# The next tile's h: root along partitions by way of DRAM, squares behind softmaxes, x loaded in pairs

## The chip, the core and the metric

One core of a Trainium2 chip runs the whole layer. The metric is the time of one execution in device microseconds (us).

## What is computed

One decoder layer on x of 2048 tokens by 1024 channels, all in float32:

```python
h = rms_norm(x, pre_norm_g)                      # h = x * rsqrt(mean(x*x) + EPS) * g, by token
proj = h @ w_in
a_u, a_v, sq, sk, sv, mq, z = jnp.split(proj, split_at, axis=-1)
y_a = chunked_spatial_gating(gelu(a_u), gelu(a_v), ...)     # group A
y_b = sliding_window_attention(sq, sk, sv, sinks, bias)     # group B, 4 heads, window 128
y_c = memory_cross_attention(mq, mk, mv)                    # group C, 4 heads, 256 memory tokens
y = jnp.concatenate([y_a, y_b, y_c], -1) * silu(z)
x = x + rms_norm(y @ w_out, post_norm_g)
```

The change touches only how h is made for the tiles of tokens after the first.

## The kernel before

The tokens are worked on in four tiles `t` of 512 (TS). `hTs` holds two tiles of h, transposed: channels along partitions in eight chunks k of 128, tokens along the free axis. Every float32 operand of a big product is split into a rounded part (made on ACT) and the rest (made on DVE), and a product of 8 chunks is 24 matmuls. So h takes three steps a chunk: a first step on DVE (x times g times the token's root), a rounding on ACT, a subtraction on DVE.

A tile runs through *units* of the weights: V (four banks of PSUM, `vps`), SV, K, Q, MQ, then eight Z and four U. After each quarter of a unit from the second Q on, `slot()` is called. Slots are numbered through the tile, 68 in tile 0 and 60 in the others, and a slot issues the jobs that a table put there, and the next stage of an attention unit. The attention of a tile is 12 units: n = 0 to 3 windows (names with `_b`), then `3_1` and the like for head 3, half 1 of the memory attention (`_c`). A unit has three stages, some slots apart: the logits `l_c`, their maximum `nm_c`, exp and normalised `L_c`; the transposes `tp_c` and their split `pT_c`; the product `o_c` and its sum `OC`. For t > 0 the eight memory units begin at slots 27, 30 and so on to 48, their transposes stand 7 slots later and their products 11. These small products, and the broadcast below, share four buffers of PSUM (`ps_t`) in turn; the units share four others.

PE and SP run in the order in which the program is written. The instructions of DVE, ACT and POOL are ordered by a scheduler that goes by its own estimate of when each is ready; within an engine they then run strictly in that order. `queue_aside` sets a few instructions straight behind a softmax. SP issues nearly all DMAs, in order: where one has to wait for its data or its buffer, those behind it wait as well. A load of weights (`whl`) waits for the buffer of the unit before, so SP keeps pace with PE unit by unit. Stores of results (`yd`, from the tiles `Z_z` and `a`) and of prepared weights of the last layer part (`wo_...`) are issued some slots after their data are due (`store_later`). The prepared weights are made in the hT that the next tile will use, so each of its chunks is free only when a store has read it.

For the next tile's h, `token_stats` loads 512 by 512 pieces of x's rows (`xs`, eight of 128 x 512, two buffers of the tag `xk`) and squares each on ACT with a sum over the row. The square has no fixed place on ACT. `rms_rstd` makes the root of the sums (`rsa_x` on DVE, `rsr_x` on POOL), a number per token along partitions. `along` turns it into a row on all partitions: four broadcasts and transposes on PE into a PSUM buffer (`bc`), copied by DVE to `bcs`. Then `load_h` loads chunk by chunk of x transposed (`xk`, the same two buffers) and makes h. In tiles t > 0 the pieces start at slots 22 to 36, the broadcast stands at slot 46, the chunks at 47 to 57; in tile 0 at 40 to 54, 58, and 59 to 66. All eight chunks are made before V of the next tile.

Of the kernel before, what the change touches and what calls it, by code (L numbers as in the profile page):

```python
# [15 lines left out]
P = 128  # L16
# [19 lines left out]
STORE_AFTER = 6  # L36
TURN_SLOT = 30
A_SLOTS0, A_SLOTS = (14, 5, 8, 13, 33, 8, 13), (7, 5, 8, 13, 27, 7, 11)


@with_exitstack
def kernel(
# [33 lines left out]
    def f32(ap):  # L76
        return ap.bitcast(F32)

    def split(hi, lo, src, lo_engine=None):
        nc.scalar.copy(hi, src)  # L80
        (lo_engine or nc.vector).tensor_tensor(lo, src, f32(hi), ALU.subtract)  # L81
# [101 lines left out]

    def token_stats(t):

        ss = tiny.tile([P, 4], F32, tag="ss", name=f"ss_{t}")
        if t > 0:
            parts = tiny.tile([P, 2, 4], F32, tag="ss2", name=f"ss2_{t}")
            for i in range(4):
                for c in range(2):  # L190
                    xs = sp.tile([P, TS], F32, tag="xk", name=f"xs_{t}_{i}_{c}", bufs=2)
                    nc.sync.dma_start(xs, x[t * TS + i * P : t * TS + (i + 1) * P, c * 512 : c * 512 + 512])
                    nc.scalar.activation(xs, xs, AF.Square, accum_out=parts[:, c, i : i + 1])
                    if i < 3 or c == 0:
                        yield
            nc.vector.tensor_tensor(ss, parts[:, 0], parts[:, 1], ALU.add)
            yield rms_rstd(ss, D, EPS, f"x{t}", "x")
            return
# [8 lines left out]
        yield rms_rstd(ss, D, EPS, f"x{t}", "x")  # L207

# [9 lines left out]

    def split_h(xk, t, k, bcs):

        hT = hTs[t % 2]
        g = g_pre[:, k : k + 1]
        if bcs is None:
            nc.scalar.mul(hT[:, 0, k, :], xk, g)
            nc.vector.scalar_tensor_tensor(hT[:, 1, k, :], xk, g, f32(hT[:, 0, k, :]), ALU.mult, ALU.subtract)
        else:
            nc.vector.scalar_tensor_tensor(xk, xk, g, bcs, ALU.mult, ALU.mult)
            split(hT[:, 0, k, :], hT[:, 1, k, :], xk)
# [174 lines left out]
    def window_unit(t, c, S, O, done):  # L403
# [27 lines left out]
        for h in range(4):  # L431
            last = nc.scalar.activation(Lc[:, h, : P + 1], Lc[:, h, : P + 1], AF.Exp, bias=nm[:, h : h + 1],  # L432
                                        accum_out=den[:, h : h + 1])
# [32 lines left out]
    def memory_unit(t, h, cc, S, O, done):  # L466
# [14 lines left out]
        for e in range(2):  # L481
            scale = late["rstd"][:, 2 * cc + e : 2 * cc + e + 1] if t == 0 else 1.0
            last = nc.scalar.activation(p[:, e, :], lg[:, e, :], AF.Exp, bias=nm[:, e : e + 1], scale=scale,  # L483
                                        accum_out=den[:, e : e + 1])
# [90 lines left out]
    def first_sums(place):  # L575
# [606 lines left out]
```

## Time and profile before

| | before |
|---|---|
| time, median of 3 runs (lowest to highest) | 785.67 us (781.81 to 788.67) |
| the profiled execution's own time | 783.76 us |
| its span, and what lies around it | 781.8 us, 1.96 us |
| granted clock of PE over the span | 0.996 |
| PE busy | 759.6 us, 97% of the span |
| DVE, ACT, POOL busy | 73%, 51%, 20% |
| DMA | 199.48 MB, mean 255 GB/s |

The tiles begin with V at 5, 174, 322 and 472 us of the span; the last product begins at 618 us. A row of the timeline has the start in us from the beginning of the span, the length of the merged piece, the engine, the line, the operation, what it writes and reads, its shape, and how many instructions; in brackets stands how long the engine was idle before it and what it waited for. Matmuls are pipelined, so that the time that one takes from the others is the step from start to start, and the same goes for DVE. A row of waits has the total, the number and the longest. A row of DMA issues ends with the median time from issue to landing.

### The profile page before, as it was taken

The numbers are of one execution on the slowest core, as the hardware profiler recorded it, in microseconds if no ns is written. First come the engines' busy times: TensorE is split into PE (matmuls) and PEld (weight loads), VectorE is DVE, ScalarE is ACT, GpSimd is POOL, SyncE is SP. The second block draws the span as 40 slices with busy tenths as digits, with TensorE's granted clock in tenths as the row PEclk, the third lists the DMA queues.
The fourth block names the chain that finished last, engine by engine and source line by source line (L and its number), as shares of the span: only waits on it lengthen the run. The fifth ranks groups of instructions, "written<-read, shape, count | busy, mean of one in ns | idle before, by whom it ended". The sixth has DMA issues, their size and how long they took to land.

```text
span 781.8 us, 10715 instructions
## 1 busy us (share of the span) xinstructions
PE 759.6 (97%) x3788; PEld 638.2 (82%) x3788; DVE 567.6 (73%) x1052; ACT 397.4 (51%) x879; POOL 157.8 (20%) x141
## 2 busy tenths in 40 slices
PE   8999999899999999999999999999999999999994
PEld 7878987787888888888887788888888878888883
DVE  6497998795658789744796796748976325697787
ACT  7686666653654656355455553544434233343442
POOL 4565543220502210041031000201300000010013
PEclk9999999999999999999999999999999999999998
DMA  8856557736875996947989769864464699818717
GB/s 326 296 205 245 184 204 256 272 123 273 314 261 210 320 316 227 343 165 224 371 292 309 260 218 379 339 261 161 142 216 178 237 388 402 322 55 322 270 32 291
DMA packets 54133, 199.48 MB, mean 255 GB/s; under 512 B 5275, under 2 KB 5824, under 8 KB 43840
## 3 DMA queue, kind: packets, MB, share of 16 engines
q1 hardware_dynamic: 53552, 198.20, 70.1%
q8 instruction: 30, 0.49, 0.2%
q10 hardware_dynamic: 528, 0.59, 0.2%
q14 instruction: 23, 0.19, 0.1%
HBM read 142.15 MB, written 56.63 MB: 254 GB/s over the span
## 4 chain that ended last, share of the span: by engine, by line
PE 70%; DMA 13%; DVE 11%; ACT 3%; issue 2%; POOL 1%; SPq 0%; POOLq 0%; DVEq 0%; ACTq 0%
PE g_z L247 14%; PE v L674 9%; PE g_u L247 7%; PE Y_S L1030 6%; PE Y L1030 5%; PE g_q L247 4%; PE g_mq L247 4%; DMA xs<-in_x 4%; PE X L1030 3%; PE X_S L1030 3%; DMA yd<-Z_z 2%; DMA split_d<-whl 2%; PE g_sv L247 2%; PE g_k L247 2%; PE gm L351 1%
## 5 line engine op out<-in xcount | busy, mean ns | idle before, releaser
L247 PE MATMUL g_z<-hT,whl 128*128 128x512 f32 x768 | 193.7, 396 | 0.0
L247 PEld LDWEIGHTS g_z<-hT,whl 128*128 128x128 f32 x768 | 138.3, 188 | 25.0
L81 POOL TENSOR_TENSOR whl<-wraw,whl 128x1024 fp32r<-128x1024 f32 x30 | 73.6, 2456 | 139.8 <-ACT whl L80 92.8
L247 PE MATMUL g_u<-hT,whl 128*128 128x512 f32 x384 | 97.7, 396 | 0.0
L674 PE MATMUL v<-whl,hT 128*128 128x512 f32 x384 | 88.9, 391 | 2.2 <-DVE sc_z L254 1.7
L674 PEld LDWEIGHTS v<-whl,hT 128*128 128x128 f32 x384 | 71.6, 188 | 18.6 <-DVE sc_z L254 2.1
L247 PEld LDWEIGHTS g_u<-hT,whl 128*128 128x128 f32 x384 | 69.2, 188 | 12.7
L80 ACT CAST whl<-wraw 128x1024 fp32r<-128x1024 f32 (+1 forms) x39 | 40.0, 1027 | 25.5 <-DMA wraw<-in_wst 6.8
L928 POOL TENSOR_TENSOR r<-a,mhalf 128x1 f32<-128x1 f32 x16 | 13.7, 856 | 191.1 <-DVE a L926 178.2
L447 POOL TENSOR_SCALAR_AFFINE_SELECT pp_b<-po_b 128x512 fp32r<-128x512 f32 x30 | 19.9, 663 | 143.3 <-ACT po_b L80 143.3
L247 PE MATMUL g_q<-hT,whl 128*128 128x512 f32 x192 | 45.9, 394 | 0.0
L1030 PE MATMUL Y<-hT,yop 128*128 128x512 f32 x192 | 44.5, 391 | 0.8 <-DVE yop L903 0.8
L247 PE MATMUL g_mq<-hT,whl 128*128 128x512 f32 x192 | 44.7, 389 | 0.0
L1030 PE MATMUL Y_S<-hT,yop_S 128*128 128x512 f32 x192 | 44.2, 389 | 0.0
L1030 PEld LDWEIGHTS Y<-hT,yop 128*128 128x128 f32 x192 | 35.8, 188 | 9.2 <-DVE yop L903 1.7
L1030 PEld LDWEIGHTS Y_S<-hT,yop_S 128*128 128x128 f32 x192 | 36.0, 188 | 7.5
L247 PEld LDWEIGHTS g_q<-hT,whl 128*128 128x128 f32 x192 | 35.7, 188 | 7.8 <-issue 0.5
L247 PEld LDWEIGHTS g_mq<-hT,whl 128*128 128x128 f32 x192 | 35.9, 188 | 7.3
L483 ACT ACTIVATE L_c<-l_c,nm_c 128x256 f32<-128x256 f32 x48 | 22.3, 469 | 28.7 <-DVE nm_c L478 28.6
L432 ACT ACTIVATE Lc_b<-Lc_b,nm_b 128x129 f32<-128x129 f32 x64 | 25.1, 394 | 18.9 <-DVE nm_b L430 18.8
L157 POOL TENSOR_TENSOR rsr_v<-rsa_v,mhalf 128x4 f32<-128x4 f32 x16 | 17.4, 1090 | 82.0 <-DVE rsa_v L155 74.1
L704 ACT ACTIVATE vhat<-G_v,nb,rsr_v 128x128 f32<-128x128 f32 x64 | 26.4, 485 | 11.5 <-DVE nb L702 11.4
(209 smaller groups left out, 1477.2 us busy)
## 6 DMA issues: line engine op xcount, KB each, us to landing
whl<-split_d SPq DMA_DIRECT2D x54, 1024.0 KB, 6.3
split_d<-whl SPq DMA_DIRECT2D x22, 1024.0 KB, 8.3
wraw<-in_wst SPq DMA_DIRECT2D x37, 512.0 KB, 5.8
hT<-wo_B SPq DMA_DIRECT2D x10, 1024.0 KB, 9.3
wo_T<-hT SPq DMA_DIRECT2D x8, 1024.0 KB, 7.8
xr<-in_x SPq DMA_DIRECT2D x16, 512.0 KB, 8.6
y<-yd SPq DMA_DIRECT2D x7, 1024.0 KB, 13.2
xs<-in_x SPq DMA_DIRECT2D x24, 256.0 KB, 6.3
```

Source lines behind the costliest of these rows:

```text
L80: nc.scalar.copy(hi, src)
L81: (lo_engine or nc.vector).tensor_tensor(lo, src, f32(hi), ALU.subtract)
L157: nc.gpsimd.tensor_tensor(r, a, mhalf[:, :c], ALU.pow)
L247: nc.tensor.matmul(ps, w[:, wi, k * P : (k + 1) * P], hT[:, hi, k, :], start=(n == 0), stop=(n == 3 * KC - 1))
L351: nc.tensor.matmul(ps, w[:, wi, k * P : (k + 1) * P], mT[:, hi, k, :], start=(n == 0), stop=(n == 3 * KC - 1))
L432: last = nc.scalar.activation(Lc[:, h, : P + 1], Lc[:, h, : P + 1], AF.Exp, bias=nm[:, h : h + 1], accum_out=den[:, h : h + 1])
L447: nc.gpsimd.affine_select(prev[:, s], f32(own[:, s]), [[0, 4], [-1, P]], ALU.is_gt, 0.0, base=0, channel_multiplier=1)
L483: last = nc.scalar.activation(p[:, e, :], lg[:, e, :], AF.Exp, bias=nm[:, e : e + 1], scale=scale, accum_out=den[:, e : e + 1])
L674: nc.tensor.matmul(vps[i], hT[:, hi, 2 * j + kk, i * P : (i + 1) * P], w[:, wi, kk * 512 : (kk + 1) * 512], start=(j == 0 and (hi, wi, kk) ...
L704: nc.scalar.activation(vhat[:, i, g, :], G[:, g * P : (g + 1) * P], AF.Identity, bias=nb[:, g : g + 1], scale=rv[:, g : g + 1])
L928: nc.gpsimd.tensor_tensor(r, a, mhalf2[:, 0:1], ALU.pow)
L1030: nc.tensor.matmul(banks[m], a(s, k)[:, m * P : (m + 1) * P], w(v, k), start=first and n == 0, stop=n == 11, skip_group_check=not first)
```

## The change

- **Root.** `rstd_d` in DRAM takes the root (`to_dram`), and a DMA that reads its row once for each partition brings it back as `bcs` (`from_dram`). The four matmuls `bc` and the copy on DVE are gone. To make the row run along the tokens, the rows of x are dealt to partitions so that partition p has tokens 4p to 4p + 3.
- **Squares.** Each square is issued four slots after its load, and placed on ACT behind the newest exp (`issue_after`). The loads start at slot 17 (tile 0: 28) instead of 22 (40); the root is at slot 38 (49), the store of it at 40 (51), the load at 43 (54).
- **x.** Chunks 0 and 1, 2 and 3, 6 and 7 are loaded as pairs of 512 KB (`xj`) into the tiles S0, S1 and S0 that the q of this tile has left; chunks 4 and 5 go singly into `xk`. So six chunks can be on their way at once. `LOADS` and `MAKES` give the slots.
- **The last made beside V.** The makes of chunks 6 and 7 (tile 0: 4 to 7) are issued after the first (tile 0: and second) quarter of the next tile's V; only those DVE and ACT instructions, in the program's order, since the scheduler then places them.

```diff
+NEXT_STATS = (28, 17)
+LOADS = ((50, 50, 53, 53, 55, 57, 65, 65), (40, 40, 42, 42, 45, 47, 55, 55))
+MAKES = ((59, 61, 63, 65, -28, -28, -24, -24), (48, 50, 52, 54, 58, 59, -28, -28))
...
+    rstd_d = dram.tile([NT, TS], F32, name="rstd_d")
+    def next_stats(t):
+        r = {}
+        parts = tiny.tile([P, 2, 4], F32, tag="ss2", name=f"ss2_{t}")
+        def load(n):
+            i, c = divmod(n, 2)
+            r[n] = sp.tile([P, TS], F32, tag="xk", name=f"xs_{t}_{n}", bufs=2)
+            rows = x[t * TS : (t + 1) * TS].rearrange("(p i) d -> p i d", i=4)
+            nc.sync.dma_start(r[n], rows[:, i, c * 512 : c * 512 + 512])
+        def square(n):
+            i, c = divmod(n, 2)
+            with tc.issue_after(late["exp"].ins):
+                nc.scalar.activation(r[n], r[n], AF.Square, accum_out=parts[:, c, i : i + 1])
+        def rstd():
+            ss = tiny.tile([P, 4], F32, tag="ss", name=f"ss_{t}")
+            nc.vector.tensor_tensor(ss, parts[:, 0], parts[:, 1], ALU.add)
+            r["rstd"] = rms_rstd(ss, D, EPS, f"x{t}", "x")
+        def to_dram():
+            nc.sync.dma_start(rstd_d[t].rearrange("(p i) -> p i", i=4), r["rstd"])
+        def from_dram():
+            late["bcs", t] = sp.tile([P, TS], F32, tag="bcs", name=f"bcs_{t}", bufs=2)
+            nc.sync.dma_start(late["bcs", t], rstd_d[t : t + 1].broadcast_to([P, TS]))
+        for n in range(8):
+            yield (0, 2, 5, 7, 10, 12, 15, 17)[n], lambda n=n: load(n)
+            yield (0, 2, 5, 7, 10, 12, 15, 17)[n] + 4, lambda n=n: square(n)
+        yield 21, rstd
+        yield 23, to_dram
+        yield 26, from_dram
...
-    def load_h(t, k, bcs):
-        xk = sp.tile([P, TS], F32, tag="xk", name=f"xk_{t}_{k}", bufs=2)
-        nc.sync.dma_start(xk, xT[t, k])
-        split_h(xk, t, k, bcs)
+    def load_x(t, k):
+        if k in (4, 5):
+            raw_x[k] = sp.tile([P, TS], F32, tag="xk", name=f"xk_{t}_{k}", bufs=2)
+            nc.sync.dma_start(raw_x[k], xT[t, k])
+        elif k % 2 == 0:
+            a = sp.tile([P, 2, TS], F32, tag="S1" if k == 2 else "S0", name=f"xj_{t}_{k}", bufs=1)
+            nc.sync.dma_start(a, xT[t, k : k + 2].rearrange("k p n -> p k n"))
+            raw_x[k], raw_x[k + 1] = a[:, 0], a[:, 1]
+    def make_h(t, k):
+        hT, xk = hTs[t % 2], raw_x.pop(k)
+        nc.vector.scalar_tensor_tensor(xk, xk, g_pre[:, k : k + 1], late["bcs", t], ALU.mult, ALU.mult)
+        split(hT[:, 0, k, :], hT[:, 1, k, :], xk)
...
-            for i in range(8):
-                jobs.setdefault(s_stats + 2 * i, []).append(stats_next)
-            jobs.setdefault(s_along, []).append(along_next)
+            for s, job in next_stats(t + 1):
+                jobs.setdefault(NEXT_STATS[t > 0] + s, []).append(job)
             for k in range(KC):
-                jobs.setdefault(s_along + 1 + int(step * k), []).append(lambda k=k: load_h(t + 1, k, late["bcs_next"]))
+                for s, f in ((LOADS[t > 0][k], load_x), (MAKES[t > 0][k], make_h)):
+                    (jobs if s >= 0 else carried).setdefault(s, []).append(lambda k=k, f=f, t=t: f(t + 1, k))
```

Tile 0's own sums and h (`first_stats`, `first_h`) stay as they were. Lines in the rows below are those of the kernel in question; with the change the same code stands further down: L81 becomes L85, L227 L272, L486 L526, L817 L849.

**First place: DVE at the end of tile 1**, from the maximum of unit 3_0 on (tile 2 has the same). `hT` rows write h or a prepared weight, `xk` and `xj` rows are first steps of makes, `a_2`, `e_u_2` and `G_u_2` belong to the third gate. Before:

```order
L478 TENSOR_REDUCE nm_c_3_0_3026<-l_c_3_0_3020 128x2
L485 RECIPROCAL den_c_3_0_3027<-den_c_3_0_3027 128x2
L486 TENSOR_TENSOR L_c_3_0_3025<-L_c_3_0_3025,den_c_3_0_3027 128x512
L534 TENSOR_TENSOR wo_0_2771<-wo_0_2771,wo_0_2230 128x512 x2
L216 COPY bcs_3046<-bc_3041 128x512
L81 TENSOR_TENSOR pT_c_2_0_3053<-tp_c_2_0_3048,pT_c_2_0_3053 128x512
L508 SCALAR_TENSOR_TENSOR e_u_2_3062<-e_u_2_3062,g_u_2_2999 128x512
L227 SCALAR_TENSOR_TENSOR xk_0_3076<-xk_0_3076,colt,bcs_3046 128x512
L814 SCALAR_TENSOR_TENSOR a_2_3073<-sg_2_3068,g_v,addend 128x512
```

With the change, from the same maximum:

```order
L518 TENSOR_REDUCE nm_c_3_0_3026<-l_c_3_0_3020 128x2
L272 SCALAR_TENSOR_TENSOR xj_0_2924<-xj_0_2924,colt,bcs_2985 128x512 x2
L272 SCALAR_TENSOR_TENSOR xj_2_2956<-xj_2_2956,colt,bcs_2985 128x512 x2
L525 RECIPROCAL den_c_3_0_3027<-den_c_3_0_3027 128x2
L85 TENSOR_TENSOR pT_c_2_0_3046<-tp_c_2_0_3041,pT_c_2_0_3046 128x512
L85 TENSOR_TENSOR hT_91<-xj_0_2924,hT_91 128x512
L846 SCALAR_TENSOR_TENSOR a_2_3066<-sg_2_3061,g_v,addend 128x512
L548 SCALAR_TENSOR_TENSOR e_u_2_3055<-e_u_2_3055,g_u_2_2997 128x512
```

The first steps of chunks 0 to 3 now stand straight behind the maximum, ahead of the normalisation of unit 3_0 and of the split of 2_0; before, the first of them stood behind both.

**The same stretch, its end**: the normalisation `L_c` of the last unit, 3_1. Before it is the 22nd instruction of the stretch, the maximum counted as the first: 17 of full width (128x512, or a maximum over it), two `OC`, and three small ones (a reciprocal and the like).

```order
L81 TENSOR_TENSOR pT_c_2_1_3132<-tp_c_2_1_3127,pT_c_2_1_3132 128x512
L485 RECIPROCAL den_c_3_1_3110<-den_c_3_1_3110 128x2
L501 TENSOR_TENSOR OC_2898<-o_c_2_0_3146,oh_c_2_0_3151 64x256
L486 TENSOR_TENSOR L_c_3_1_3108<-L_c_3_1_3108,den_c_3_1_3110 128x512
L81 TENSOR_TENSOR hT_91<-wo_0_2771,hT_91 128x512
```

With the change it is the 34th: 28 of full width (six of them first steps of makes, and one step of the gate of the same form), three `OC`, and three small ones.

```order
L85 TENSOR_TENSOR pT_c_3_0_3167<-tp_c_3_0_3162,pT_c_3_0_3167 128x512
L849 TENSOR_TENSOR a_2_3066<-a_2_3066,G_u_2_3059 128x512
L525 RECIPROCAL den_c_3_1_3098<-den_c_3_1_3098 128x2
L85 TENSOR_TENSOR hT_91<-xk_5_3069,hT_91 128x512
L541 TENSOR_TENSOR OC_2889<-o_c_2_1_3176,oh_c_2_1_3181 64x256
L852 TENSOR_TENSOR a_2_3066<-a_2_3066,Z_z_2_3146 128x512
L526 TENSOR_TENSOR L_c_3_1_3096<-L_c_3_1_3096,den_c_3_1_3098 128x512
```

It moved behind the makes of chunks 0 to 5, the split of 3_0 and the steps of the third gate.

**Second place: SP at the same time**, from the store of the second gate's result on. `whl` rows are loads of weights, `wo_...` stores of prepared weights. Before:

```order
L531 DMA yd<-a_1_2755 128x512
L531 DMA yd<-Z_z_4_2408 128x512
L531 DMA yd<-Z_z_5_2482 128x512
L531 DMA wo_T_85<-hT_91 256x1x1024
L123 DMA whl_13_2997<-split_d 128x2048
```

With the change:

```order
L571 DMA yd<-a_1_2746 128x512
L228 DMA rstd_d<-rsr_x_2880 128x4
L267 DMA xj_0_2924<-in_xT 128x2x512
L571 DMA yd<-Z_z_4_2400 128x512
L571 DMA yd<-Z_z_5_2476 128x512
L267 DMA xj_2_2956<-in_xT 128x2x512
L571 DMA wo_T_85<-hT_91 256x1x1024
L232 DMA bcs_2985<-rstd_d 128x512
L127 DMA whl_13_2995<-split_d 128x2048
```

The store of the root and the first pair of x stand ahead of two stores of `yd`, and the load of `bcs` and the second pair ahead of the next weights.

**Third place: DVE at the end of tile 0.** First, behind the split of a weight (`whl_0`). Before:

```order
L81 TENSOR_TENSOR whl_0_1654<-wraw_0_1561,whl_0_1654 128x1024
L508 SCALAR_TENSOR_TENSOR e_u_2_1632<-e_u_2_1632,sc_u_2_1630 128x512
L501 TENSOR_TENSOR OC_1448<-o_c_1_1_1646,oh_c_1_1_1651 64x256
L81 TENSOR_TENSOR pT_c_2_1_1672<-tp_c_2_1_1667,pT_c_2_1_1672 128x512
L758 SCALAR_TENSOR_TENSOR Z_z_6_1458<-OC_1448,Z_z_6_1458 128x512
```

With the change:

```order
L85 TENSOR_TENSOR whl_0_1664<-wraw_0_1576,whl_0_1664 128x1024
L272 SCALAR_TENSOR_TENSOR xj_0_1537<-xj_0_1537,colt,bcs_1616 128x512 x2
L272 SCALAR_TENSOR_TENSOR xj_2_1600<-xj_2_1600,colt,bcs_1616 128x512
L548 SCALAR_TENSOR_TENSOR e_u_2_1640<-e_u_2_1640,sc_u_2_1638 128x512
L272 SCALAR_TENSOR_TENSOR xj_2_1600<-xj_2_1600,colt,bcs_1616 128x512
L541 TENSOR_TENSOR OC_1458<-o_c_1_1_1656,oh_c_1_1_1661 64x256
L272 SCALAR_TENSOR_TENSOR xk_4_1654<-xk_4_1654,colt,bcs_1616 128x512
L85 TENSOR_TENSOR pT_c_2_1_1682<-tp_c_2_1_1677,pT_c_2_1_1682 128x512
```

Five first steps of makes now stand between the split and pT_c of unit 2_1. Second, the copy `sc_z_3` that frees the last gate's PSUM buffer, which is the fourth bank of the next V. Before:

```order
L508 SCALAR_TENSOR_TENSOR e_u_3_1791<-e_u_3_1791,sc_u_3_1789 128x512
L227 SCALAR_TENSOR_TENSOR xk_4_1805<-xk_4_1805,colt,bcs_1692 128x512
L501 TENSOR_TENSOR OC_1448<-o_c_3_0_1829,oh_c_3_0_1834 64x256
L511 SCALAR_TENSOR_TENSOR G_u_3_1795<-e_u_3_1791,sc_u_3_1789 128x512
L81 TENSOR_TENSOR hT_92<-xk_4_1805,hT_92 128x512
L817 TENSOR_TENSOR a_3_1802<-a_3_1802,G_u_3_1795 128x512
L254 TENSOR_TENSOR sc_z_3_1865<-g_z_3_1816,bcs_486 128x512
```

With the change:

```order
L541 TENSOR_TENSOR OC_1458<-o_c_3_0_1813,oh_c_3_0_1818 64x256
L548 SCALAR_TENSOR_TENSOR e_u_3_1782<-e_u_3_1782,sc_u_3_1780 128x512
L294 TENSOR_TENSOR sc_z_3_1844<-g_z_3_1805,bcs_488 128x512
L551 SCALAR_TENSOR_TENSOR G_u_3_1786<-e_u_3_1782,sc_u_3_1780 128x512
L849 TENSOR_TENSOR a_3_1793<-a_3_1793,G_u_3_1786 128x512
```

The copy moved from behind two steps of a make and two of the gate to straight behind `e_u_3`.

More of the change, by code (lines that the diff above doesn't have):

```diff
@@ L180, with first_stats @@
     g_pre, g_mem = colt[:, 0:8], colt[:, 8:16]
[L184 to L198, printed above, removed]
+    def first_stats():
+        ss = tiny.tile([P, 4], F32, tag="ss", name="ss_0")
         for i in range(4):
@@ L217, in along, with first_h @@
         return bcs
-    def split_h(xk, t, k, bcs):
-        hT = hTs[t % 2]
+    def first_h(xk, k):
         g = g_pre[:, k : k + 1]
[L223 to L228, printed above, removed]
-    def load_h(t, k, bcs):
-        xk = sp.tile([P, TS], F32, tag="xk", name=f"xk_{t}_{k}", bufs=2)
-        nc.sync.dma_start(xk, xT[t, k])
-        split_h(xk, t, k, bcs)
+        hT = hTs[0]
+        nc.scalar.mul(hT[:, 0, k, :], xk, g)
+        nc.vector.scalar_tensor_tensor(hT[:, 1, k, :], xk, g, f32(hT[:, 0, k, :]), ALU.mult, ALU.subtract)
+    raw_x = {}
+    def load_x(t, k):
[10 more added lines that the diff above has]
+        split(hT[:, 0, k, :], hT[:, 1, k, :], xk)
     late = {}
@@ L431, in window_unit @@
         for h in range(4):
-            last = nc.scalar.activation(Lc[:, h, : P + 1], Lc[:, h, : P + 1], AF.Exp, bias=nm[:, h : h + 1],
+            last = late["exp"] = nc.scalar.activation(Lc[:, h, : P + 1], Lc[:, h, : P + 1], AF.Exp, bias=nm[:, h : h + 1],
                                         accum_out=den[:, h : h + 1])
@@ L482, in memory_unit @@
             scale = late["rstd"][:, 2 * cc + e : 2 * cc + e + 1] if t == 0 else 1.0
[L483 removed]
+            last = late["exp"] = nc.scalar.activation(p[:, e, :], lg[:, e, :], AF.Exp, bias=nm[:, e : e + 1], scale=scale,
                                         accum_out=den[:, e : e + 1])
```

15 lines of the change are left out of this document (5 added, 10 removed).

## The prediction

> **What bounds the kernel now.** I read the shares first, then three windows, then the waits of PE, then the timeline of each engine around each wait.
>
> ```profile
> PE 759.6 (97%) x3788; PEld 638.2 (82%) x3788; DVE 567.6 (73%) x1052; ACT 397.4 (51%) x879; POOL 157.8 (20%) x141
> ...
> 12.00:771.20 759.20, 749.47 (x3746) 630.17 (x3746) 555.26 (x1033) 388.09 (x866) 150.04 (x129) 1.00 0.71 255
> ```
>
> The first column of a windows row is its length, the second PE's busy time. Between the first operands and the last product PE is idle for 759.20 - 749.47 = 9.7 us, at full granted clock (1.00). So PE bounds the kernel, and the change can win at most those 9.7 us and the PE time that it takes out. The waits of PE say where they are:
>
> ```profile
> PE o_c L497 <- DVE OC L501: 1.7, 2, 1.4
> PE l_c L473 <- DVE nm_c L480: 1.7, 1, 1.7
> PE v L674 <- DVE sc_z L254: 1.7, 1, 1.7
> ...
> PE o_c L497 <- DVE pT_c L81: 1.5, 1, 1.5
> PE tp_c L491 <- DVE pT_c L81: 1.2, 1, 1.2
> ```
>
> All stand in the second halves of tiles 0 and 2, the last hundred us of a tile or less. Tile 1 has none: there the same program just keeps up.
>
> **What goes: the broadcast on PE.** Its time is the step from its start to the next instruction's, since matmuls overlap.
>
> ```profile
> 297.30 1.05 PE L213 MATMUL bc<-ident,rsr_x 128*128 128x128 f32 x8
> 298.19 0.60 PE L491 MATMUL tp_c<-ident,L_c 128*128 128x128 f32 x4
> ...
> 315.63 0.60 PE L491 MATMUL tp_c<-ident,L_c 128*128 128x128 f32 x4
> ```
>
> 298.19 - 297.30 = 0.89 us of PE in tile 1, where PE never waits; by the neighbours of the other two it is as much or less, so I take 0.85 x 3 = **2.5 us**, all on the path.
>
> **What goes: squares that hold ACT.** ACT takes its instructions in order, and in the kernel before a square stood there before its chunk of x had landed.
>
> ```profile
> 127.76 0.63 ACT L193 ACTIVATE xs<-xs 128x512 f32<-128x512 f32 x1 [2.42 <-DMA xs<-in_x]
> 129.83 0.71 PE L473 MATMUL l_c<-MK,S_mq 128*128 128x256 f32 x4 [1.68 <-DVE nm_c L480]
> 428.19 0.63 ACT L193 ACTIVATE xs<-xs 128x512 f32<-128x512 f32 x1 [3.12 <-DMA xs<-in_x]
> 430.16 0.74 PE L497 MATMUL o_c<-pT_c,MV 128*128 128x256 f32 x4 [1.50 <-DVE pT_c L81]
> 442.41 0.60 ACT L517 ACTIVATE Z_z<-g_z 128x512 f32<-128x512 f32 x1 [3.51 <-DMA yd<-Z_z]
> 447.30 0.66 PE L491 MATMUL tp_c<-ident,L_c 128*128 128x128 f32 x4 [1.18 <-DVE pT_c L81]
> ```
>
> Each of the first two PE waits follows 2 us behind a square that waited for its load. The third follows Z_z, which waited for a store that the second delay had made late; it waits for a PSUM buffer, and without bc the turn of four buffers gives it an older one. The load now stands four slots ahead of its square. The two tp_c rows above are of slots 46 and 55, so a slot takes (315.63 - 298.19) / 9 = 1.94 us, and four take 7.8. Against it stands the time to landing:
>
> ```profile
> xs<-in_x SPq DMA_DIRECT2D x24, 256.0 KB, 6.3
> DMA to landing us min/median/max: 3.3/6.3/8.8
> ```
>
> the data are there at the median. I count 1.68 + 1.50 + 1.18 = **4.4 us** as gone; bounds 0 (the longest landing, 8.8, is over 7.8) and 4.4.
>
> **What goes: the wait ahead of the next tile's V.** PE's fourth bank of V waited for a copy on DVE, which stood behind a make of h and two steps of the gate:
>
> ```profile
> 176.26 0.74 DVE L227 SCALAR_TENSOR_TENSOR xk<-xk,colt,bcs 128x512 f32<-128x512 f32 x1
> ...
> 179.30 0.68 DVE L254 TENSOR_TENSOR sc_z<-g_z,bcs 128x512 f32<-128x512 f32 x1
> 180.04 17.98 PE L674 MATMUL v<-whl,hT 128*128 128x512 f32 x78 [1.68 <-DVE sc_z L254]
> ```
>
> By the order after the change sc_z stands straight behind e_u, ahead of the makes, so it ends 2 us or more earlier: **1.7 us** gone. Together 2.5 + 4.4 + 1.7 = 8.6 us. The waits at o_c behind OC (1.4) I leave: DVE stood beside POOL there, and the change doesn't move that.
>
> **What comes: makes that stand early on DVE, ends of tiles 1 and 2.** The scheduler sets four makes straight behind the maximum of unit 3_0, and moves the last normalisation, L_c of unit 3_1, behind them. In tile 1 before:
>
> ```profile
> 297.54 0.69 DVE L478 TENSOR_REDUCE nm_c<-l_c 128x2 f32<-128x512 f32 x1
> ...
> 304.56 0.42 DVE L501 TENSOR_TENSOR OC<-o_c,oh_c 64x256 f32<-64x256 f32 x1
> 305.01 0.69 DVE L511 SCALAR_TENSOR_TENSOR G_u<-e_u,g_u 128x512 f32<-128x512 f32 x1
> 305.61 0.68 DVE L478 TENSOR_REDUCE nm_c<-l_c 128x2 f32<-128x512 f32 x1
> ...
> 308.02 0.75 DVE L227 SCALAR_TENSOR_TENSOR xk<-xk,colt,bcs 128x512 f32<-128x512 f32 x1
> 308.68 0.17 DVE L416 COPY Lc_b<-sink_bc 128x4 f32<-128x4 f32 x1
> ...
> 309.75 0.67 DVE L486 TENSOR_TENSOR L_c<-L_c,den_c 128x512 f32<-128x512 f32 x1
> ```
>
> A full-width instruction takes 305.61 - 305.01 = 0.60 us of DVE, a make's first step 308.68 - 308.02 = 0.66. From 297.54 to the end of that normalisation (309.75 + 0.67 = 310.4) it took 12.9 us. After the change the same stretch holds, by the order, 28 full-width instructions instead of 17 (7 of 0.66, 21 of 0.60: 17.2 us), three of 0.45 or less on half the partitions (305.01 - 304.56) and three small ones of 0.1 (the copy at 308.68 is one): 18.8 us, 5.9 more. PE's transposes of that L_c came 315.63 - 310.4 = 5.2 us later, and come 0.85 sooner without bc: 4.4 us of cover. So PE waits 5.9 - 4.4 = 1.5 us there, although two of eight makes have left the stretch. The store of yd is now issued behind rstd_d, near 289.9 (worked out below) instead of 285.43, and Z_z waits for it on ACT as at 442.41. That delay of 4.5 us is mostly covered, since Z_z now stands behind two exps and two casts more; of its bounds, 0 and 4.5, I take 0.5, near the wait of 0.99 that tile 1 had there at no cost to PE. So **2.0 us** each; from below nothing, since two makes less may leave DVE ahead, and 6 from above.
>
> **What comes: the way over DRAM.** The first make waits for bcs, and behind it on DVE stand pT_c, L_c and the gates that PE needs. SP can't issue bcs before rstd_d has landed. No row shows this pair, so it is bounded by neighbours:
>
> ```profile
> 287.14 1.37 POOL L157 TENSOR_TENSOR rsr_x<-rsa_x,mhalf 128x4 f32<-128x4 f32 x1 [12.82 <-DVE rsa_x L155]
> 284.00:292.00 8.00, 8.00 (x46) 6.78 (x45) 6.88 (x16) 4.89 (x15) 1.37 (x1) 1.00 1.01 354
> 285.43 1.19 SPq L531 DMA_DIRECT2D yd<-Z_z  x2
> 292.10 0.60 ACT L517 ACTIVATE Z_z<-g_z 128x512 f32<-128x512 f32 x1 [0.99 <-DMA yd<-Z_z]
> sink_bc<-in_sinks SPq DMA_DIRECT2D x1, 2.0 KB, 8.2
> out<-oa ACTq DMA_DIRECT2D x2, 256.0 KB, 2.2
> DMA to landing us min/median/max: 2.4/3.8/9.5
> ```
>
> The root is ready at 287.14 + 1.37 = 288.5; two DVE instructions now stand ahead of rsa_x, so 289.5. Ahead of bcs SP issues rstd_d (0.4 us) and 2.5 MB (two xj, two yd, wo_T); at 354 GB/s, the rate with the DMA engines full (1.01), they take 7.1 us, and bcs ends no sooner than the shortest landing of 256 KB, 2.2: 289.5 + 0.4 + 7.1 + 2.2 = 299.2. DVE asks for it at 297.54 + 0.5 + 0.6 = 298.6. I take a wait w of **0.6 us** in tiles 1 and 2. Below, it is 0; above, 8.2 (a small transfer, sink_bc) plus 9.5 (the longest xk) give 307.2, so w = 8.6. PE waits w longer, since there is no cover left.
>
> The Trainium skill, page "DMA: Bandwidth & Descriptors", section "Latency and other measured facts", puts most of a fixed cost of about 2 us per DMA on the receipt from memory, which speaks against two transfers in a row where one PE broadcast stood. An estimate by that figure alone, two times 2 us behind 289.5, would have bcs there by 294 and w at 0, and the sum 1.2 us lower. This trace doesn't go that way: the pair of yd, issued at 285.43 to 286.6, landed at 292.1, so the queue ahead sets it.
>
> **Tile 0.** Here bcs is asked for later, behind the split of whl on DVE, so I put w at 0. Five first steps stand newly ahead of pT_c of unit 2_1:
>
> ```profile
> 159.16 0.69 DVE L81 TENSOR_TENSOR pT_c<-tp_c,pT_c 128x512 fp32r<-128x512 f32 x1
> 162.62 2.62 DVE L227 SCALAR_TENSOR_TENSOR xk<-xk,colt,bcs 128x512 f32<-128x512 f32 x2
> 163.08 0.64 PE L497 MATMUL o_c<-pT_c,MV 128*128 128x256 f32 x4
> 161.19 2.84 POOL L81 TENSOR_TENSOR whl<-wraw,whl 128x1024 fp32r<-128x1024 f32 x1 [7.64 <-ACT whl L80]
> ```
>
> 5 x 0.66 = 3.3 us, against a cover of 163.08 - 159.85 - 0.85 = 2.4: **0.9 us**; 0 from below. Two makes beside POOL took 2.62 instead of 1.4, so 2.1 from above. The skill's page "SBUF — State Buffer", section "Who interferes with whom", says that a DVE instruction with two SBUF inputs contends with a GpSimd one that reads SBUF; the 2.62 agrees, and 2.1 instead of 0.9 would be the sum's only change.
>
> **The sum.** -8.6 + 2 x (2.0 + 0.6) + 0.9 = -2.5 us. The profiled execution took 783.76 (span 781.8), so 781.3; it lies 1.9 under the median of 785.67, whose three runs reach from 781.81 to 788.67. The forecast is 783.0, by the median 785.67 - 2.5 = 783.2. About 1% (7.9 us) is what a measurement of this kernel can tell from no change.
>
> **Rivals.** *The makes fit in.* If the 1.5 and 0.9 are covered after all and bcs is in time, the 8.6 stay: 777.1. For it: in tile 1 DVE kept PE fed. Against: it had hardly an idle us there (6.88 of 8.00). *The broadcast lands late.* DVE stands at the first make in every tile, and each us of w is a us of PE, three times: -8.6 + 4.0 + 0.9 + 3w. It is slower than before from w = 1.2 on, by 1% from 3.9; at 5 us it gives 797. For it: DMA engines full, a median of yd of
>
> ```profile
> yd<-Z_z SPq DMA_DIRECT2D x16, 256.0 KB, 9.2
> ```
>
> Against: the queue drained in 6 to 7 us in tile 1. *The squares still wait*, since SP blocks ahead of their loads: then the 4.4 stay, and 783.0 becomes 787.4.
>
> **Chances.** Forecast 0.57 (780 to 787), makes fit in 0.17, late broadcast 0.12, squares still wait 0.14. Faster by over 1% is the second alone, 0.17; slower is the third, 0.12; the rest, 0.71, within 1%. The range holds all but the late broadcast and a tail: 776 to 792.
>
> **What would show it.** Right: no bc on PE; no waits of xs on ACT; no wait at the first bank of V of tile 1; waits of 1 to 3 us at the last tp_c or o_c of tiles 1 and 2, for L_c or pT_c. Wrong: DVE idle for bcs longer than 2 us, or PE without waits at the ends of tiles. An unforeseen wait at V for h of chunks 6 and 7, or for Z_z of the last gate behind their makes, would spoil it.

## The result, and the profile after

The changed kernel takes 795.34 us (median of four runs, 791.60 to 796.94) against 784.69 us before on the same chip (781.81 to 788.67): a ratio of 1.0126, with a 95% interval from 1.0093 to 1.0159. It is slower by 10.7 us, outside the predicted range of 776 to 792. The profiled execution took 795.36 us, with a span of 793.5 us instead of 781.8.

The busy times on the page, and then what PE waited for (total us, times, longest us):

```profile
PE 760.9 (96%) x3764; PEld 637.7 (80%) x3764; DVE 568.3 (72%) x1049; ACT 395.6 (50%) x879; POOL 157.6 (20%) x141
```

```profile
PE tp_c L531 <- DVE pT_c L85: 4.4, 2, 2.2
PE sg L844 <- DVE OC L541: 3.0, 1, 3.0
PE tp_c L531 <- DVE L_c L526: 3.0, 2, 1.5
PE o_c L537 <- ACT L_c L523: 2.7, 2, 1.7
...
PE Y L1062 <- ACT yop L929: 1.4, 1, 1.4
```

PE has 24 matmuls less (3788 before): the broadcast, eight records a tile, is gone. Its busy time isn't lower, since a part of tile 0 ran at half clock (below). The other engines are busy about as long as before. The loss is waits: those at `tp_c` and `o_c`, 10.1 us, come in pairs, one in tile 1 and one in tile 2; `sg` is the end of tile 0; `Y` is the first product of the last part.

Tile 1, as SP issued it in the changed kernel (start, duration, and what was issued):

```profile
287.94 0.38 SPq L571 DMA_DIRECT2D yd<-a  x1
292.51 0.32 SPq L228 DMA_DIRECT2D rstd_d<-rsr_x  x1
292.88 0.63 SPq L267 DMA_DIRECT2D xj<-in_xT  x1
293.92 0.79 SPq L571 DMA_DIRECT2D yd<-Z_z  x2
294.77 0.46 SPq L267 DMA_DIRECT2D xj<-in_xT  x1
295.33 1.06 SPq L571 DMA_DIRECT2D wo_T<-hT  x1
296.87 0.33 SPq L232 DMA_DIRECT2D bcs<-rstd_d  x1
```

The same stretch by windows of the changed kernel (start:end, length, PE, PEld, DVE, ACT, POOL, granted clock, share of the DMA engines, GB/s):

```profile
292.50:296.90 4.40, 4.40 (x26) 3.75 (x25) 3.24 (x8) 2.77 (x8) 0.00 (x0) 1.00 0.40 119
296.90:301.00 4.10, 4.10 (x25) 3.50 (x24) 2.30 (x4) 1.81 (x5) 0.00 (x0) 1.00 1.06 412
```

SP stood from 288.3 to 292.5 for the root, so nothing was queued behind it; then it needed 4.4 us to issue the six transfers ahead of `bcs`, and meanwhile the DMA engines were 40% busy. What DVE did (the bracket names what it sat idle for):

```profile
302.17 0.69 DVE L518 TENSOR_REDUCE nm_c<-l_c 128x2 f32<-128x512 f32 x1
305.64 2.74 DVE L272 SCALAR_TENSOR_TENSOR xj<-xj,colt,bcs 128x512 f32<-128x512 f32 x4 [2.78 <-DMA bcs<-rstd_d]
...
323.12 0.68 DVE L526 TENSOR_TENSOR L_c<-L_c,den_c 128x512 f32<-128x512 f32 x1
```

DVE sat 2.78 us for `bcs` (3.11 in tile 2), with `pT_c` and `L_c` behind it. Behind that PE waited at four places of this tile, 5.1 us in all.

Tile 0, first on DVE, then on POOL, then on PE:

```profile
157.25 2.08 DVE L272 SCALAR_TENSOR_TENSOR xj<-xj,colt,bcs 128x512 f32<-128x512 f32 x3 [0.58 <-DMA bcs<-rstd_d]
...
162.34 4.09 DVE L85 TENSOR_TENSOR hT<-xj,hT 128x512 fp32r<-128x512 f32 x3
...
168.75 0.41 DVE L541 TENSOR_TENSOR OC<-o_c,oh_c 64x256 f32<-64x256 f32 x1
```

```profile
162.85 2.43 POOL L85 TENSOR_TENSOR whl<-wraw,whl 128x1024 fp32r<-128x1024 f32 x1 [14.33 <-ACT whl L84]
```

```profile
169.22 2.08 PE L844 MATMUL sg<-wsp,vhat 128*128 128x128 f32 x8 [3.04 <-DVE OC L541]
...
179.47 2.91 PE L706 MATMUL v<-whl,hT 128*128 128x512 f32 x12
```

```profile
169.00:171.00 2.00, 1.78 (x9) 1.78 (x9) 2.00 (x5) 1.88 (x4) 0.00 (x0) 0.50 0.04 8
```

DVE had sat 0.58 us for `bcs` here too, and from there to `OC` it had no gap. Three second steps of makes took 4.09 us, 1.36 each on average instead of 0.6; POOL's split of a weight ran beside them for 2.43 us of that. `OC` stood behind them, and PE waited 3.0 us for it. After that wait the granted clock was 0.50. From `sg` to the first product of V went 179.47 - 169.22 = 10.25 us. In the kernel before, the same stretch, at full clock, was 174.09 - 166.76 = 7.33:

```profile
166.76 1.05 PE L812 MATMUL sg<-wsp,vhat 128*128 128x128 f32 x8
...
174.09 4.27 PE L674 MATMUL v<-whl,hT 128*128 128x512 f32 x18
```

So the end of tile 0 lost 3.0 us by the wait and 2.9 by the clock.

### The profile page after: what moved, and what is told of

The parts are those of the page before. It is cut to its first block, busy times and chain, and to the rows that moved or that the text cites. A ratio compares the mean times of both kernels' runs of the same rounds, so it can differ in the third digit from the quotient of the medians.

```text
span 793.5 us, 10650 instructions
## 1 busy us (share of the span) xinstructions
PE 760.9 (96%) x3764; PEld 637.7 (80%) x3764; DVE 568.3 (72%) x1049; ACT 395.6 (50%) x879; POOL 157.6 (20%) x141
## 4 chain that ended last, share of the span: by engine, by line
PE 71%; DVE 12%; DMA 10%; issue 3%; ACT 3%; POOL 1%; POOLq 0%; SPq 0%; DVEq 0%; ACTq 0%
PE g_z L287 14%; PE v L706 10%; PE g_u L287 6%; PE g_q L287 6%; PE g_mq L287 5%; PE Y L1062 5%; PE Y_S L1062 4%; DMA bcs<-rstd_d 3%; PE g_sv L287 3%; PE g_k L287 3%; PE X_S L1062 3%; PE X L1062 2%; PE l_b L462 2%; DVE hT L85 2%; DMA xs<-in_x 2%
## 5 line engine op out<-in xcount | busy, mean ns | idle before, releaser
L85 POOL TENSOR_TENSOR whl<-wraw,whl 128x1024 fp32r<-128x1024 f32 x30 | 74.4, 2483 | 142.9 <-ACT whl L84 142.7
L487 POOL TENSOR_SCALAR_AFFINE_SELECT pp_b<-po_b 128x512 fp32r<-128x512 f32 x30 | 20.4, 680 | 144.6 <-ACT po_b L84 144.6
L935 DVE TENSOR_TENSOR yop<-y,yop 128x1024 fp32r<-128x1024 f32 x12 | 14.6, 1219 | 27.2 <-ACT yop L929 27.2
```

The costliest lines, as they stand in the source:

```text
L487: nc.gpsimd.affine_select(prev[:, s], f32(own[:, s]), [[0, 4], [-1, P]], ALU.is_gt, 0.0, base=0, channel_multiplier=1)
L935: nc.vector.tensor_tensor(w[:, 1, ks], yraw[name, p][:, ks], f32(w[:, 0, ks]), ALU.subtract)
```

## The experiments

Theory: the loss in tiles 1 and 2 is the late broadcast and the early place of the makes on DVE together. Rivals: the broadcast alone, DVE's order alone, or neither but the traffic. Each time is a median, beside that of the kernel before on the same chip.

**Makes late in tiles 1 and 2.** `late["pT"]` is the last step of the latest `pT_c` in the program's order.

```diff
+        with tc.issue_after(late["pT"].ins) if t > 1 else nullcontext():
             nc.vector.scalar_tensor_tensor(xk, xk, g_pre[:, k : k + 1], late["bcs", t], ALU.mult, ALU.mult)
             split(hT[:, 0, k, :], hT[:, 1, k, :], xk)
```

> The changed kernel with its broadcast by DRAM and all its loads as they are; only in tiles 1 and 2 each make of h (both its DVE steps) is held on DVE behind the last pT_c that stands ahead of it in the program, so pT_c of unit 2_0 and L_c of unit 3_0 come first and the makes are spread between the later ones. The traces put 5.7 us of PE waits at the end of tile 1 and 6.0 at the end of tile 2. Theory 'broadcast and order' (2.8 and 3.1 us of them are DVE idle for bcs, the other 2.9 each the eight steps ahead of pT_c and L_c): both go, 795.3 becomes about 784. Theory 'broadcast alone': the makes ask some 2.5 us later, so w falls to 0.5 and the time to about 785 as well. Rival 'traffic' (the waits come of SP held for the root and of loads that collide, whatever DVE's order): no more than 2 us better, 793 to 795.

Measured: 783.22 us, before 784.25; ratio 0.9993 (0.9976 to 1.0011). The waits of PE in this run, from the longest on:

```profile
PE sg L845 <- DVE OC L542: 3.0, 1, 3.0
PE Y L1063 <- ACT yop L930: 1.8, 1, 1.8
PE o_c L538 <- DVE OC L542: 1.6, 1, 1.6
```

Those of tiles 1 and 2 are gone; tile 0's stays. 12.1 us came back, and those waits account for 10.1 of them; traffic alone is out. What share the broadcast has, this run can't say, since the makes now ask for it later.

**Broadcast early, makes early.**

```diff
-NEXT_STATS = (28, 17)
+NEXT_STATS = (28, 15)
...
-            nc.sync.dma_start(rstd_d[t].rearrange("(p i) -> p i", i=4), r["rstd"])
+            (nc.gpsimd if t > 1 else nc.sync).dma_start(rstd_d[t].rearrange("(p i) -> p i", i=4), r["rstd"])
...
-            nc.sync.dma_start(late["bcs", t], rstd_d[t : t + 1].broadcast_to([P, TS]))
+            (nc.gpsimd if t > 1 else nc.sync).dma_start(late["bcs", t], rstd_d[t : t + 1].broadcast_to([P, TS]))
...
+        with tc.issue_after(late["nm", 3, 0].ins) if t > 1 and k < 4 else nullcontext():
             nc.vector.scalar_tensor_tensor(xk, xk, g_pre[:, k : k + 1], late["bcs", t], ALU.mult, ALU.mult)
```

> The changed kernel with the makes of tiles 1 and 2 as early on DVE as they are (the four first steps straight behind nm_c of unit 3_0, ahead of pT_c of unit 2_0), but the store of the root and the broadcast of tiles 2 and 3 on POOL's DMA queue, behind nothing, and their squares two slots sooner, so that bcs is there before it is asked for; L_c of unit 3_1 stands four steps sooner. Theory 'broadcast and order': the 2.8 and 3.1 us for bcs go, 2 to 3 us each at tp_c and o_c stay: about 789. Theory 'broadcast alone': 11.7 us go: about 784. Theory 'order alone': DVE is as late for pT_c as before: 793 to 795.

Measured: 786.67 us, before 784.25; ratio 1.0030 (1.0016 to 1.0045). POOL's row of the two transfers in tile 1, and DVE's of the makes:

```profile
285.17 0.73 POOL L228 DMA_DIRECT2D rstd_d<-rsr_x  x1 [0.32 <-POOL rsr_x L161]
291.14 0.56 POOL L232 DMA_DIRECT2D bcs<-rstd_d  x1 [5.25 <-DMA rstd_d<-rsr_x]
```

```profile
301.37 2.73 DVE L272 SCALAR_TENSOR_TENSOR xj<-xj,colt,bcs 128x512 f32<-128x512 f32 x4
```

No bracket: `bcs` was there. PE waited nowhere at the ends of tiles 1 and 2. This came between the numbers of my theory (789) and of "broadcast alone" (784), so the order's share wasn't settled: `L_c` of unit 3_1 is the 31st instruction of the stretch here, three steps sooner than in the changed kernel, which the next run takes back.

**The same, with `L_c` back in its place.** The makes of chunks 6 and 7 are also held, behind the product of `a` and U. This kernel does not compute the layer rightly. I put that to an operand of the last part's weights that is written over h in the buffer that they share, which no run shows. PE, DVE and ACT run as many instructions as in the changed kernel, so it serves for their timing.

```diff
+        put_off = t in (1, 2) and (h, cc) == (3, 1)
+        if not put_off:
+            norm()
         yield
+        if put_off:
+            with tc.issue_after(late["az"].ins), tc.issue_after(late["OC"].ins):
+                norm()
```

> As the run with the broadcast on POOL's queue (786.7 us, no PE wait at the ends of tiles 1 and 2), with one thing moved back: the normalisation L_c of unit 3_1 stands again behind pT_c of unit 3_0, OC of 2_1 and both products of a, as in the changed kernel, so that the stretch from nm_c of 3_0 to it holds the prediction's 18.8 us of DVE, with bcs on time. In the run before, nm_c of 3_0 ended at 301.4 us, and PE without waits wants that L_c by about 318.2. The prediction's term: 301.4 + 18.8 = 320.2, so PE waits 2.0 us at tp_c for L_c in each of the tiles 1 and 2: 790 to 791. Rival 'the makes fit in' (without the wait for bcs DVE keeps up even in this order): 786 to 787.

Measured: 788.96 us, before 784.49; ratio 1.0053 (1.0031 to 1.0074). DVE's stretch in tile 1, and PE's waits in tiles 1 and 2:

```profile
298.28 0.69 DVE L518 TENSOR_REDUCE nm_c<-l_c 128x2 f32<-128x512 f32 x1
...
316.36 0.68 DVE L527 TENSOR_TENSOR L_c<-L_c,den_c 128x512 f32<-128x512 f32 x1
```

```profile
317.18 0.63 PE L538 MATMUL tp_c<-ident,L_c 128*128 128x128 f32 x4 [1.10 <-DVE L_c L527]
```

```profile
465.77 0.63 PE L538 MATMUL tp_c<-ident,L_c 128*128 128x128 f32 x4 [2.10 <-DVE L_c L527]
```

From 298.28 to 316.36 + 0.68 = 317.04 are 18.76 us, the 18.8 of the prediction. PE waits 1.1 and 2.1 us at the place that it named, so the makes don't fit in. The time is less than the 790 to 791 expected, and its interval overlaps that of the run before, so the order's share is read from the two profiles: tile 1 is 1.3 us longer here, and tile 2 2.3 (the table below). Theory "broadcast and order" stands, with this part of the order at 1 to 2 us a tile and the broadcast at more. The broadcast's part isn't quite its own: with the store on POOL, SP no longer stands for the root and issues the loads behind it sooner, and no run parts the two.

**Makes late in tile 0.** The same pin, for `t == 1`.

> The changed kernel with the makes of tile 0 alone held behind pT_c in the same way; tiles 1 and 2 as in the changed kernel. There PE waited 0.5 us for pT_c and 3.0 us for OC at the gate's sg, and then ran some 5 us at half the granted clock. Theory 'order': those 3.5 us go and the clock doesn't fall, together 5 us: about 790. Rival 'SP' (SP stood 9 us for the root of tile 1 and then issued weights late): no change, 795. Rival 'moved on' (the makes then stand ahead of the copies that V's banks wait for): half comes back at V, 793.

Measured: 790.66 us, before 784.25; ratio 1.0079 (1.0058 to 1.0101); 4.7 us better than the changed kernel. Its rows of PE, and the window of the half clock:

```profile
165.36 1.05 PE L845 MATMUL sg<-wsp,vhat 128*128 128x128 f32 x8
...
172.69 4.27 PE L707 MATMUL v<-whl,hT 128*128 128x512 f32 x18
179.37 6.89 PE L707 MATMUL v<-whl,hT 128*128 128x512 f32 x29 [2.41 <-DVE sc_z L295]
```

```profile
169.00:171.00 2.00, 2.00 (x10) 1.65 (x10) 2.00 (x4) 1.29 (x3) 2.00 (x1) 1.00 1.03 226
```

The wait at `sg` is gone, the clock stays at 1.00, and `sg` to V takes 7.33 us again. SP's rival falls. "Moved on" is right as well: V's fourth bank waits for `sc_z` again, 2.4 us. DVE's rows there, in this run and then in the changed kernel:

```profile
176.71 0.68 DVE L549 SCALAR_TENSOR_TENSOR e_u<-e_u,sc_u 128x512 f32<-128x512 f32 x1
177.31 1.41 DVE L273 SCALAR_TENSOR_TENSOR xj<-xj,colt,bcs 128x512 f32<-128x512 f32 x2
178.64 0.68 DVE L295 TENSOR_TENSOR sc_z<-g_z,bcs 128x512 f32<-128x512 f32 x1
```

```profile
179.19 0.69 DVE L294 TENSOR_TENSOR sc_z<-g_z,bcs 128x512 f32<-128x512 f32 x1 [1.75 <-PE g_z L287]
```

The pin of this run put two makes between `e_u` and `sc_z`. In the changed kernel `sc_z` stood straight behind `e_u`, and DVE sat idle for the product that it reads.

**The squares' part alone.** The kernel before, with the earlier loads and the pinned squares, chunks and makes as they were, and the broadcast on PE.

```diff
-        yield 23, to_dram
-        yield 26, from_dram
+        yield (30 if t == 1 else 29), broadcast
```

> The kernel before, with the earlier loads of x for the squares and the squares held behind softmaxes four slots later, and nothing else of the change: the broadcast on PE, single chunks of x, all makes in their old slots. By the prediction's step the PE waits at 430 and 447 us go, as they did in the changed kernel (1.5 and 1.2), the one at 130 stays as it did there (1.5): 2.7 us less than before, about 782. Rival 'the squares still wait' (SP blocks ahead of their loads): the same as before, 784 to 785.

Measured: 781.82 us, before 784.25; ratio 0.9968 (0.9949 to 0.9988), as expected. What ACT waited for at the squares, before and in this run:

```profile
ACT xs L193 <- DMA xs<-in_x: 21.4, 13, 3.1
```

```profile
ACT xs L220 <- DMA xs<-in_x: 7.8, 3, 4.3
```

Ten of 13 waits are gone. The PE waits at 430 and 447 us go with them; that at 130 us stays (1.9 us in this run), and a new one of 1.4 us stands at `tp_c` in tile 1, for `pT_c`.

**All makes late.** The pin for every tile, and for tile 0's chunks 4 to 7 behind the last `sc_z`.

```diff
+        with tc.issue_after(late["sc" if t == 1 and k > 3 else "pT"].ins):
```

> The changed kernel with the makes held late in all three tiles, behind pT_c; in tile 0 those of chunks 4 to 7 behind the last sc_z, for which V's fourth bank waited 2.4 us when they stood ahead of it. If the parts add up: 783.2 (tiles 1 and 2) less 4.7 (tile 0) less 2.4 (V) = about 776, 1% below the kernel before. Rival 'given back at V': chunks 4 to 7 come too late for V's third and fourth unit, and 2 us or more come back there: 778 or more.

Measured: 782.62 us, before 784.49; ratio 0.9983 (0.9966 to 1.0001). The parts don't add up: 776 was expected. The waits at `sg` and V are gone as planned, but the start of tile 1 has new ones, of which these are two of four rows:

```profile
208.41 0.66 PE L772 MATMUL svt<-ident,svs 128*128 128x128 f32 x4 [1.10 <-ACT svs L758]
...
226.57 0.50 PE L463 MATMUL l_b<-KK,S_q 128*128 128x256 f32 x2 [0.84 <-DVE S_q L433]
```

The work of the four chunks was moved into V's time, and ACT and DVE came late behind it. "Given back" was right, a few units later than I had placed it; but the four waits are 2.4 us of the 6.6 that are missing. In this profile PE also ran the first products of the last part's `Y` at half the granted clock for some 3.4 us, and took about 1 us longer from there on than with makes late in tiles 1 and 2; the rest is open.

**The same with the broadcast on PE.**

> The same with the broadcast on PE and the copy on DVE, as before the change, in place of the way over DRAM; squares, loads and the place of the makes unchanged. By the prediction's first term the 24 products of the broadcast cost 2.5 us of PE: 778.6 against 776. Rival 'the way over DRAM has a price elsewhere': all four kernels that go over DRAM wait 1.5 to 1.9 us at the first product of the last part, for the cast of y, the two that don't go there wait none; if the way itself does that, 776.8. Rival 'free': if the PE broadcast hides in PE's waits, 776 or less.

Measured: 781.64 us, before 784.49; ratio 0.9964 (0.9947 to 0.9980), no slower than over DRAM, and not the 778.6 expected. Of its PE waits, none is at the last part for the cast `yop` on ACT. So in this setting what the way over DRAM saves on PE is lost elsewhere.

**Squares and the way over DRAM**, chunks and makes as before.

> The kernel before with two parts of the change: the squares' part (781.8 alone) and the way over DRAM by SP's queue; single chunks of x, and all makes in their old slots, the first behind pT_c of unit 2_0. If the DRAM way is only PE time saved: 781.8 less 2.5 = 779.3. If it also brings the wait at the last part: 781. If bcs is still late at the first make (it lands near 302 and is asked for about then), each us of that costs one or two in tiles 1 and 2: 783 or more.

Measured: 779.93 us, before 784.49; ratio 0.9938 (0.9920 to 0.9957). The lowest time of all kernels here. Its interval just overlaps that of the squares alone (0.9949 to 0.9988); the two kernels below repeat the pair, and differ by 2.0 us as these do by 1.9. SP's rows in tile 1, and the longest wait of PE:

```profile
287.21 0.32 SPq L228 DMA_DIRECT2D rstd_d<-rsr_x  x1
287.97 0.79 SPq L571 DMA_DIRECT2D yd<-Z_z  x2
288.86 1.88 SPq L571 DMA_DIRECT2D wo_T<-hT  x1
291.58 0.33 SPq L232 DMA_DIRECT2D bcs<-rstd_d  x1
```

```profile
PE Y L1062 <- ACT yop L929: 2.2, 1, 2.2
```

Without the pairs of x (1 MB) ahead of it, `bcs` lands 6.4 to 7.6 us after its issue, instead of 8.7 to 9.2, and the first make, at 301.85, doesn't wait. So the way over DRAM cost time in the changed kernel by what stood ahead of it in the queue and by what was put behind it on DVE, and not by itself.

**The wait at the last part**, two kernels.

```diff
+            for ps in (slice(0, P),) if t == 1 else (slice(0, 64), slice(64, P)):
+                nc.sync.dma_start(late["bcs", t][ps], rstd_d[t : t + 1].broadcast_to([ps.stop - ps.start, TS]))
```

> The run with the squares' part and the way over DRAM (779.9 us), with one edit: the broadcast of tiles 2 and 3 comes in two DMAs of 64 partitions each, so that SP's queue carries eight DMAs more than before the change instead of six; all engines' orders are the same. It is for the wait at the first product of the last part, 1.4 to 2.4 us in every kernel that goes over DRAM, none in the three that don't, though nothing of the change is left in that part. Theory 'turn of eight' (the program's semaphores for DMAs go round by eight, and with them the place of the last loads): with eight more the wait goes, 777.5 to 778. Rival 'the way itself' (addresses, traffic): it stays, 780.

```diff
+        def to_dram():
+            for n in range(2):
+                nc.sync.dma_start(rstd_d[(t + n) % NT].rearrange("(p i) -> p i", i=4), r["rstd"])
```

> The squares' part alone (781.8 us, broadcast on PE), with six small DMAs added and nothing that reads them: the root of tiles 1, 2 and 3 is stored to DRAM twice, 2 KB each, by SP. Theory 'turn of eight': the wait of about 2 us at the last part's first product comes, 784. Rival 'the way itself' (it needs the broadcast): none, 782. SP is held for the root here too; if that costs, it shows as later loads in tiles 0 to 2 and not in the last part.

Measured: 780.40 us (ratio 0.9941, 0.9920 to 0.9962) and 782.37 us (0.9962, 0.9942 to 0.9981), before 784.51. The row in the first, and in the second:

```profile
PE Y L1063 <- ACT yop L930: 1.2, 1, 1.2
```

```profile
PE Y L1062 <- ACT yop L929: 1.0, 1, 1.0
```

With eight more DMAs the wait stays, so "turn of eight" falls; with stores of the root and no broadcast it comes too, so the rival that needs the broadcast falls as well. All nine profiled kernels that store the root to DRAM wait 1.0 to 2.2 us there, the three that don't wait none. The traces show one step more: the cast waits for the load of y, and SP holds that load until the last stores of `yd` have landed. In the nine SP stands 8.5 to 10.2 us for them, in the three 7.9 to 8.0. Why those stores land later is open.

## Why the prediction was wrong, point by point

The direction came out as the rival "the broadcast lands late", but not by that alone. The parts of a profiled execution, from PE's first product of V in a tile to the next, and of the last part, in us (tile 3 takes 145.1 to 145.4 in all):

| | tile 0 | tile 1 | tile 2 | last part up to `Y` | from `Y` on |
|---|---|---|---|---|---|
| before | 168.7 | 148.4 | 149.6 | 21.8 | 142.8 |
| changed | 174.1 | 151.4 | 151.4 | 23.3 | 142.9 |
| makes late in tiles 1 and 2 | 173.1 | 145.3 | 145.7 | 23.7 | 143.2 |
| broadcast early | 174.0 | 146.3 | 146.3 | 23.5 | 144.6 |
| the same, `L_c` back | 171.1 | 147.5 | 148.6 | 23.5 | 144.1 |
| makes late in tile 0 | 167.4 | 153.5 | 151.2 | 23.5 | 143.1 |
| squares alone | 169.0 | 149.8 | 146.4 | 21.8 | 142.7 |
| all makes late | 167.2 | 149.2 | 145.4 | 23.3 | 144.2 |
| squares and DRAM | 167.1 | 147.7 | 146.0 | 24.2 | 142.8 |

By the prediction's steps:

- **Broadcast on PE, 2.5 us.** It went from PE. Between the two runs with squares the way over DRAM gained 781.8 - 779.9 = 1.9 us net, with up to 2.2 us lost again at the last part, a place that the prediction didn't look at.
- **Squares, 4.4 us.** Mis-sized: 2.4 us measured alone. Two of the three waits went, as argued, and tile 2 is 3.1 us shorter, but tile 1 is 1.4 us longer by its new wait. At 130 us PE waited 1.7 us before, 1.3 in the changed kernel and 1.9 with the squares alone, now for `pT_c` and not for `nm_c`. No square stood ahead of it: in the changed kernel ACT sat 3.6 us, until 122.3, for the store of a prepared weight, DVE's `e_u` behind it took 2.5 us, and from there to that `pT_c` DVE had next to no gap.
- **V's fourth bank, 1.7 us.** Right, as far as the runs show. In the changed kernel `sc_z` stood where the prediction had it, and PE didn't wait. Tile 0 was late there, which could hide a wait; but with all makes late, where the makes stand behind `sc_z` and PE doesn't wait at `sg`, V waits 0.3 us and not 1.7. The 2.4 us with makes late in tile 0 came of that run's own order.
- **Makes early on DVE, 2.0 us a tile.** Right: 18.8 us forecast, 18.76 measured with `bcs` on time, and waits of 1.1 and 2.1 us. In the changed kernel the stretch took 323.12 + 0.68 - 302.17 = 21.63 us, 18.8 and the wait of 2.78.
- **The wait w, 0.6 us a tile.** This step failed. The root was ready about when forecast, since SP stood until then. But the 7.1 us for 2.5 MB took a rate of 354 GB/s from a window in which the queue was full. Here SP had just stood 4.2 us, the queue had run low, and for 4.4 us it moved 119 GB/s while SP issued one transfer after the other. From the issue of the root's store to the first make went 305.64 - 292.51 = 13.1 us, not 299.2 - 289.5 = 9.7. Of these 3.4 us the slow start is a part only: `bcs` itself took 8.7 us from its issue, behind what was still on its way. DVE also asked later, 302.17 + 0.69 - 292.51 = 10.35 us behind the store instead of 9.1, since Z_z waited 2.27 us for the late store of `yd`. So w was 2.8 and 3.1 us, and PE waited some 5 us at the end of each of the two tiles instead of 2.6. With the broadcast early on POOL's queue 8.7 us came back (795.3 to 786.7), 2.3 of them by the place of `L_c`.
- **The rival "the broadcast lands late".** It had the sign right, and only part of the price. With the measured waits for `bcs`, 0.6, 2.8 and 3.1 us, its own sum gives -8.6 + 4.0 + 0.9 + 6.5 = 2.8 us slower; the span grew by 11.7. Its chance, 0.12, was too low: the argument against it, a queue that drained in 6 to 7 us, was read from a stretch in which SP didn't wait.
- **Tile 0, 0.9 us, at most 2.1.** This step failed as badly. At the place named, `o_c` behind `pT_c`, PE waited 0.5 us. But I followed DVE only to `pT_c`. Behind it stood the second steps of three makes, beside POOL, ahead of an `OC` whose bank PE needed: 3.0 us, and 2.9 more at half clock, together 6.4 us. The wait for `bcs`, put at 0 here, was 0.6 us, and DVE had no gap behind it. With the makes of this tile late, tile 0 is 6.7 us shorter, and tile 1 2.1 longer.
- **Last part, nothing.** 1.4 us in the trace; cause open.

By the trace: -2.5 (broadcast) - 2.7 (squares) - 1.7 (V) + 10.4 (tiles 1 and 2, with 0.3 for `pT_c` in tile 1) + 0.5 + 3.0 + 2.9 (tile 0) + 1.4 (last part) = +11.3 us, of the 11.7 by which the span grew. The forecast was -2.5. Of the 13.8 us between the two sums, tile 0 is 5.5, tiles 1 and 2 are 5.2, the squares 1.7 and the last part 1.4.

## What to carry to other kernels

A rate read from a stretch in which the queue was full doesn't hold for one that follows a wait of the engine that issues: here SP stood 4.2 us for the root, then needed 4.4 us to issue what was ahead of `bcs`, and meanwhile the DMA engines were 40% busy. So count from the end of such a wait the time to issue everything ahead, or leave less ahead: without the pairs of x, `bcs` was in time. And where work is moved ahead on an engine that feeds PE, follow the engine to every instruction that frees a bank, not only to the first.

## What the runs showed of the hardware

- **Waits of PE and the granted clock.** After the wait of 3.0 us at `sg` the granted clock was 0.50 in the profiled executions of the changed kernel and of the run with the broadcast early, for some 6.8 us, and of the run with makes late in tiles 1 and 2, for some 3.4 us. In a fourth with the same wait (`L_c` back) it stayed at 1.00. From `sg` to V it cost 2.9 us in the changed kernel and 1.7 with makes late in tiles 1 and 2. The waits of 2.2 to 2.4 us elsewhere left the clock at 1.00. But the length of a wait doesn't settle it here: at the first products of `Y`, it was at 0.50 for some 3.4 us after waits of 1.2 to 1.6 us and then 0.5, in four of the nine kernels that wait there. Those four took 143.9 to 144.6 us from `Y` on, all other kernels 142.7 to 143.2. The Trainium skill, page "TensorE: Matmul & The Clock Gate", section "Part 1: The HAM clock gate", has the clock at half after an idle window of about 3.4 us, and that window running freely. That equal waits did and didn't lower the clock agrees with a free-running window, and so do its lengths of 3.4 and 6.8 us at half; that so short waits were enough is less than the figure there.
- **DVE beside POOL.** Three steps of 128x512 took 4.09 us, with POOL's split of `whl` beside them for 2.43 us: 1.36 each on average, against 0.60. The Trainium skill, page "SBUF — State Buffer", section "Who interferes with whom", has the two contend; the traces agree.
- **A store of 2 KB and the broadcast behind it.** On POOL's queue, with nothing ahead of them there, the store took 5.7 and 5.5 us to land in tiles 1 and 2, and the broadcast of 256 KB 6.3 and 6.1; the DMA engines were 82% and then 94% busy meanwhile in tile 1. In tile 0, on SP's queue, where the DMA moved 24 GB/s, the same store landed in 1.4 us. So an empty queue of its own didn't take it past the others' traffic here; that POOL's queue is slower by itself isn't ruled out.
